# The low half of every fourth weight chunk: a ScalarE copy and an accumulating DMA in place of a VectorE subtraction

## The chip, the cores and the metric

The kernel runs on one core of a Trainium2 chip. A core has a matrix engine (TensorE; PE in the profile, its weight loads PEld), a vector engine (VectorE, DVE), a scalar engine (ScalarE, ACT), a general engine (GpSimd, POOL) and a queue engine (SyncE, SP). Each works through its own instructions in order; between engines only semaphores order the work. Sixteen DMA engines move data between the chip's main memory and the on-chip memory; SP, ACT and POOL can each hand transfers to them. The metric is device time in microseconds (us), the median of the runs, lower is better.

## The reference, cut to what matters

The reference is a two-layer decoder trunk on 256 tokens of width 2048, all in float32: layer 0 mixes retention heads with a short convolution, layer 1 is differential attention with two softmax maps per head, and each layer ends in a SwiGLU block of hidden width 5632.

```python
def swiglu(h, w_gate, w_up, w_down):
    return (jax.nn.silu(h @ w_gate) * (h @ w_up)) @ w_down
...
for layer in range(DEPTH):
    h = rms_norm(x, norm_mix[layer])
    x = x + (hybrid_retention_conv if layer % 2 == 0 else diff_attention)(h, ...)
    x = x + swiglu(rms_norm(x, norm_ffn[layer]), w_gate, w_up, w_down)
```

Nearly all arithmetic is in the products with weights: the input projection (2048 x 6144), the query-key-value projection (2048 x 6144), two output projections (2048 x 2048), and per layer gate, up (2048 x 5632 each) and down (5632 x 2048). Every weight is read once.

## The kernel before, in words

A product is cut into blocks of 512 output columns (`col_block`, L126). A block has two accumulators, one for each half of the 256 tokens, and walks along the contraction in **chunks** of 256 weight rows (two k-tiles of 128), so a block with 16 k-tiles has eight chunks (c0 = 0, 2, ... 14) and a chunk of weights is 128 partitions x 1024 numbers, 512 KB. The whole kernel has 784 chunks.

To keep float32 accuracy on a matrix engine that takes a shortened type (fp32r), activations and weights are split into a high part and a low part, and each product is made of three: high x high (L146), low activation x high weight (L147), high activation x low weight (L148). With two k-tiles and two token halves a chunk is 12 matmuls of 512 columns. The way of a chunk's weights is:

- SP issues a 1 MB load for two chunks into a `raw` buffer (L135). There are four such buffers, so a load waits until the chunks of the load four before it have been split.
- ACT writes the high part, `whi = cast(raw)` (L138). There are four `whi` buffers; the cast waits until PE has done the last matmul with the chunk four before.
- DVE writes the low part, `wlo = raw - whi` (L140), into one of four `wlo` buffers.
- PE runs the 12 matmuls (L146 to L148).

`wpool` hands its buffers out in turn, so chunks c0 = 2, 10 of a 16-tile block (every fourth chunk) always meet the same `whi` and the same `wlo` buffer. Small transposes and attention products run on PE between chunks; they come from a queue of jobs (`step`, L115). The names in the profile are block letters with `_raw`, `_hi`, `_lo`, `_a` (accumulator): `g` gate, `u` up, `d...` down, `n1o`, `n3o` output projections, `aq`, `ak`, `av` attention, `rq` to `cb` layer 0. `n_hi`, `n_lo`, `d0b_hi` are activations.

The instructions of each engine stand in the order that the program's scheduler gave them when the kernel was built; it may move an instruction ahead of another on its engine where data allow.

In attention POOL does a part of the rotary embedding: squares (L480), a power for the norm (L108) and four multiplications of 128x256 for each q or k (L491). Otherwise POOL is nearly empty.

Of the kernel before, what the change touches and what calls it, by code (L numbers as in the profile page):

```python
# [9 lines left out]
F32 = mybir.dt.float32  # L10
F32R = mybir.dt.float32r
AF = mybir.ActivationFunctionType
ALU = mybir.AluOpType
# [3 lines left out]
P = 128  # L17
# [4 lines left out]
NB = 512  # L22
KC = 2
KD = 4
# [11 lines left out]
def decoder_trunk(ctx: ExitStack, tc: tile.TileContext, a: dict):  # L36
    nc = tc.nc
# [5 lines left out]
    small = ctx.enter_context(tc.tile_pool(name="small", bufs=3))  # L43
# [5 lines left out]
    def tp_tile(name):  # L49
        return psum.tile([P, NB], F32, tag="tp", name=name, bufs=2)  # L50

# [1 line left out]
    ident = cpool.tile([P, P], F32, name="ident")  # L53
    x_sb = cpool.tile([P, NT, D], F32, name="x_sb")
    gcol = cpool.tile([P, 88], F32, name="gcol")
# [21 lines left out]
    def turn_gains(i, n):  # L77
# [8 lines left out]
        out=ident, in_=ident, compare_op=ALU.not_equal, fill=1.0, base=0,  # L86
# [13 lines left out]
            pattern=[[-1, P]], channel_multiplier=1,  # L100
        )

# [1 line left out]
    def rsqrt_mean(out, ss, n):  # L104
        """out = (ss / n + eps) ** -0.5 on small [P, w] tiles."""
        w = ss.shape[1]
        nc.vector.tensor_scalar(out, ss, 1.0 / n, EPS, ALU.mult, ALU.add)
        nc.gpsimd.tensor_tensor(out, out, mhalf[:, :w], ALU.pow)  # L108

    # Work that follows a product but holds the tensor engine runs between the chunks of the next  # L110
    # product: each job is a generator that yields where the tensor engine should go on meanwhile.
    jobs = deque()

    def step():
# [9 lines left out]
            step()  # L124

    def col_block(name, w, row0, n0, nk, hi, lo, kd=KD):  # L126
        """acc[t] = act[t] @ w[row0 : row0 + nk * P, n0 : n0 + NB], act split in hi + lo."""
        acc = [acc_tile(f"{name}_a{t}") for t in range(NT)]
        for c0 in range(0, nk, KC):
            if c0 % KD == 0:  # L130
                raw = wpool.tile([P, KD, NB], F32, tag="raw", name=f"{name}_raw{c0}", bufs=4)
            if c0 % kd == 0:
                k0 = row0 + c0 * P
                rows = w[k0 : k0 + kd * P, n0 : n0 + NB].rearrange("(k p) n -> p k n", p=P)
                nc.sync.dma_start(raw[:, c0 % KD : c0 % KD + kd], rows)  # L135
            part = raw[:, c0 % KD : c0 % KD + KC]
            whi = wpool.tile([P, KC, NB], F32R, tag="whi", name=f"{name}_hi{c0}")
            nc.scalar.copy(whi, part)  # L138
            wlo = wpool.tile([P, KC, NB], F32R, tag="wlo", name=f"{name}_lo{c0}")
            nc.vector.tensor_tensor(wlo, part, whi.bitcast(F32), ALU.subtract)  # L140
            for t in range(NT):
                ts = slice(t * P, (t + 1) * P)
                for j in range(KC):
                    k = c0 + j
                    first, last = k == 0, k == nk - 1
                    nc.tensor.matmul(acc[t], lhsT=hi[:, k, ts], rhs=whi[:, j], start=first, stop=False)  # L146
                    nc.tensor.matmul(acc[t], lhsT=lo[:, k, ts], rhs=whi[:, j], start=False, stop=False)  # L147
                    nc.tensor.matmul(acc[t], lhsT=hi[:, k, ts], rhs=wlo[:, j], start=False, stop=last)  # L148
            step()
        flush()  # L150
        return acc
# [4 lines left out]
        return hi, lo  # L156

    def split4(src, hi, lo, k0, t, name):
        """Transpose src [P tokens, 512] of token tile t into k-tiles k0 .. k0+3 of hi and lo."""
        pt = tp_tile(f"{name}_tp")  # L160
        for j in range(4):
            nc.tensor.transpose(pt[:, j * P : (j + 1) * P], src[:, j * P : (j + 1) * P], ident)
        pv = pt.rearrange("p (j s) -> p j s", j=4)
        ts = slice(t * P, (t + 1) * P)
        nc.scalar.copy(hi[:, k0 : k0 + 4, ts], pv)
        nc.vector.tensor_tensor(lo[:, k0 : k0 + 4, ts], pv, hi.bitcast(F32)[:, k0 : k0 + 4, ts], ALU.subtract)

    class Stream:
        """The residual stream's next normed activation: x * gain, transposed and split, with
        the row scale kept apart for the products' results."""  # L170

        def __init__(self, name, g0):
            self.name, self.g0 = name, g0
# [8 lines left out]
                nc.scalar.activation(junk, x_sb[:, t, cs], AF.Square, accum_out=self.ss[:, t, c : c + 1])  # L182

        def pair(self, q):
            """k-tiles 2q and 2q + 1."""
            pt = tp_tile(f"{self.name}_tp{q}")
            for j in range(2):
                k = 2 * q + j
                for t in range(NT):
                    nc.tensor.transpose(  # L190
                        pt[:, j * S + t * P : j * S + (t + 1) * P], x_sb[:, t, k * P : (k + 1) * P], ident
                    )
            for j in range(2):
                k = 2 * q + j
                g = gcol[:, self.g0 + k : self.g0 + k + 1]
                pv = pt[:, j * S : (j + 1) * S]
                nc.scalar.activation(self.hi[:, k], pv, AF.Copy, scale=g)
                nc.vector.scalar_tensor_tensor(
                    self.lo[:, k], pv, g, self.hi.bitcast(F32)[:, k], op0=ALU.mult, op1=ALU.subtract
                )  # L200
# [27 lines left out]
            nc.vector.tensor_tensor(x_sb[:, t, cs], acc[t], x_sb[:, t, cs], ALU.add)  # L228

    def rope(psum_in, r, cos, sin, out, h, hd, name):  # L230
        """out = rope(r * in) for h heads of hd columns; sin's first half carries the minus."""
        half = hd // 2
        v = psum_in.rearrange("p (h d) -> p h d", d=hd)
        ca = work.tile([P, h, hd], F32, tag="ropeA", name=name + "_A")
        cb = work.tile([P, h, hd], F32, tag="ropeB", name=name + "_B")
        nc.vector.scalar_tensor_tensor(
            ca, v, r, cos.unsqueeze(1).to_broadcast([P, h, hd]), op0=ALU.mult, op1=ALU.mult
        )
        for i in range(2):
            o, s = slice(i * half, (i + 1) * half), slice((1 - i) * half, (2 - i) * half)  # L240
            nc.vector.scalar_tensor_tensor(
                cb[:, :, o], v[:, :, s], r, sin[:, o].unsqueeze(1).to_broadcast([P, h, half]),
                op0=ALU.mult, op1=ALU.mult,
            )
        nc.gpsimd.tensor_tensor(out.rearrange("p (h d) -> p h d", d=hd), ca, cb, ALU.add)

    def transpose4(src, dst, t, name):
        """src [P tokens, 512] -> dst[:, 0:4, tokens of t], float32."""
        pt = tp_tile(f"{name}_tp")
        for j in range(4):  # L250
            nc.tensor.transpose(pt[:, j * P : (j + 1) * P], src[:, j * P : (j + 1) * P], ident)
        nc.scalar.copy(dst[:, :, t * P : (t + 1) * P], pt.rearrange("p (j s) -> p j s", j=4))
# [10 lines left out]
            yield  # L263
            split4(srcs[t], hi, lo, k0, t, f"{name}{t}")

# [1 line left out]
    st = Stream("n0", 0)  # L267
    st.pair(0)
    jobs.append(st.whole())
# [16 lines left out]
    for nm, n0, dst in (("rq", 0, qT), ("rk", 512, kT)):  # L286
        acc = proj(nm, n0, KC if n0 == 0 else KD)
# [39 lines left out]
    for half in range(2):  # L327
        acc = proj(f"rv{half}", 1024 + half * NB)
# [5 lines left out]
        acc = proj(f"rg{half}", 2048 + half * NB)  # L334
# [39 lines left out]
    for half in range(2):  # L374
        acc = proj(f"cc{half}", 4096 + half * NB)
# [3 lines left out]
        acc = proj(f"cx{half}", 5120 + half * NB)  # L379
# [3 lines left out]
        acc = proj(f"cb{half}", 3072 + half * NB)  # L383
# [45 lines left out]
    st, r = out_proj("n1", a["hyb_w_out"][0], KT, ca_hi, ca_lo, 32)  # L429
    st, r = ffn(0, st, r, 16)  # L430

# [1 line left out]
    cosa = work.tile([P, NT, AD], F32, tag="ropeA", name="cosa")  # L433
    sina = work.tile([P, NT, AD], F32, tag="ropeB", name="sina")
    nc.scalar.dma_start(cosa, a["cosa"].rearrange("(t p) d -> p t d", p=P))
# [34 lines left out]
    scale = AD ** -0.5  # L470

    def rotary(i, nm, acc, grp):
        """Norm and rotary embedding of four heads' q or k; returns both token tiles."""
        ct, sn = tabs[i]
        rots = []
        for t in range(NT):
# [20 lines left out]
        return rots  # L497

    def softmax(grp, hh, aq, ak):
        """The weights p0 / sum0 - lam * p1 / sum1 of one head: [queries, keys] of both query tiles."""  # L500
        nm = f"{grp}{hh}"
        sc = psum.tile([P, 2, NB], F32, tag="sc", name=f"asc{nm}")
        for m in range(2):
# [103 lines left out]


def _tables():
    """Rotary tables and decays: they depend on the shapes alone."""  # L610
    import numpy as np

    f32 = np.float32
    out = {}
    for nm, dim in (("r", RDK), ("a", AD)):
        inv = (f32(10000.0) ** (-np.arange(0, dim, 2, dtype=f32) / f32(dim))).astype(f32)
        ang = (np.arange(S, dtype=f32)[:, None] * inv[None, :]).astype(f32).astype(np.float64)
        c, s = np.cos(ang), np.sin(ang)
        out["cos" + nm] = np.concatenate([c, c], 1).astype(f32)
        out["sin" + nm] = np.concatenate([-s, s], 1).astype(f32)  # L620
    gamma = f32(1.0) - np.exp2(f32(-5.0) - np.arange(RH, dtype=f32)).astype(f32)
    log_g = np.log(gamma.astype(np.float64)).astype(f32).astype(np.float64)
    dist = np.arange(S)[None, :] - np.arange(P)[:, None]
    dec = np.where(dist >= 0, np.exp(log_g[:, None, None] * np.maximum(dist, 0)), 0.0) * RDK ** -0.5
    dec = dec.transpose(1, 0, 2)
    out["decay"] = np.ascontiguousarray(dec.reshape(P, RH * S)).astype(f32)
    return out
# [23 lines left out]
```

## Time and profile before

| | |
|---|---|
| median of 2 runs | 2235.55 us (2235.45 to 2235.66) |
| span of the profiled execution, first to last instruction | 2233.8 us |
| PE busy | 2224.0 us (100%) |
| DVE, ACT, POOL busy | 1235.7 (55%), 996.0 (45%), 115.8 us (5%) |
| DMA | 418.90 MB, mean 188 GB/s |
| granted TensorE clock | 1.000 |

The span is of one profiled execution, on its own clock from the first to the last instruction; the profile gives no other time for that execution. It is 1.75 us under the median. Matmuls overlap in the records (one lasts 390 ns, but the next starts after 227 ns), so PE's pace is read from starts.

### The profile page before, as it was taken

What the parts mean: (1) busy time and instruction counts of PE and PEld (TensorE: products, weight loads), DVE (VectorE), ACT (ScalarE), POOL (GpSimd) and SP (SyncE); (2) the same over time, 40 slices, a digit from 0 to 9 for tenths busy, and PEclk for the clock granted to TensorE, in tenths of its full rate; (3) what the DMA queues carried; (4) which work ended last, traced back from release to release, by engine and by line L of the source; (5) the groups of instructions that cost most, each with busy time, mean ns of one, the idle gap of its engine ahead of it and who ended that gap; (6) DMA issues with size and microseconds to landing.
All of it is one profiled execution on the core that took longest, in us unless ns stands there. A gap on an engine that the chain in (4) does not pass through costs nothing.

```text
span 2233.8 us, 25353 instructions
## 1 busy us (share of the span) xinstructions
PE 2224.0 (100%) x10115; PEld 1842.8 (82%) x10115; DVE 1235.7 (55%) x1320; ACT 996.0 (45%) x1172; POOL 115.8 (5%) x104
## 2 busy tenths in 40 slices
PE   8999999999999999999999999999999999999999
PEld 7888888888888888888888888888888888888887
DVE  5555565544554555455677778665445544554554
ACT  5444445444334443444545545554444344434443
POOL 1110000000000000000031233000000000000000
PEclk9999999999999999999999999999999999999999
DMA  8555555555565655555555555555555656555553
GB/s 286 174 180 188 191 186 188 189 189 189 189 197 192 193 190 188 189 189 188 188 177 164 188 170 170 170 188 189 189 189 189 194 190 193 191 192 189 188 188 132
DMA packets 212860, 418.90 MB, mean 188 GB/s; under 512 B 7341, under 2 KB 10885, under 8 KB 212613
## 3 DMA queue, kind: packets, MB, share of 16 engines
q1 hardware_dynamic: 209904, 414.34, 56.7%
q10 hardware_dynamic: 2836, 2.93, 0.4%
q8 instruction: 79, 1.29, 0.2%
q14 instruction: 41, 0.33, 0.0%
HBM read 415.15 MB, written 2.10 MB: 187 GB/s over the span
## 4 chain that ended last, share of the span: by engine, by line
PE 99%; DMA 1%; ACT 0%; DVE 0%; SPq 0%; issue 0%
PE g_a L146 7%; PE g_a L148 7%; PE g_a L147 7%; PE u_a L146 7%; PE u_a L147 7%; PE u_a L148 7%; PE av_a L148 1%; PE av_a L146 1%; PE ak_a L148 1%; PE n3o_a L147 1%; PE ak_a L147 1%; PE n3o_a L146 1%; PE aq_a L147 1%; PE aq_a L148 1%; PE n3o_a L148 1%; PE n1o_a L148 1%
## 5 line engine op out<-in xcount | busy, mean ns | idle before, releaser
L140 DVE TENSOR_TENSOR u_lo<-u_raw,u_hi 128x1024 fp32r<-128x1024 f32 x176 | 215.6, 1225 | 263.0 <-ACT u_hi L138 263.0
L140 DVE TENSOR_TENSOR g_lo<-g_raw,g_hi 128x1024 fp32r<-128x1024 f32 x176 | 215.6, 1225 | 226.5 <-ACT g_hi L138 224.8
L138 ACT CAST g_hi<-g_raw 128x1024 fp32r<-128x1024 f32 x176 | 185.5, 1054 | 287.3 <-PE g_a L147 139.9
L138 ACT CAST u_hi<-u_raw 128x1024 fp32r<-128x1024 f32 x176 | 185.6, 1055 | 252.0 <-PE u_a L147 132.9
L146 PE MATMUL g_a<-g_hi,n_hi 128*128 128x512 f32 x704 | 277.3, 394 | 0.0
L148 PE MATMUL g_a<-g_lo,n_hi 128*128 128x512 f32 x704 | 274.4, 390 | 0.0
L147 PE MATMUL g_a<-g_hi,n_lo 128*128 128x512 f32 x704 | 273.9, 389 | 0.0
L146 PE MATMUL u_a<-u_hi,n_hi 128*128 128x512 f32 x704 | 273.9, 389 | 0.0
L147 PE MATMUL u_a<-u_hi,n_lo 128*128 128x512 f32 x704 | 273.9, 389 | 0.0
L148 PE MATMUL u_a<-u_lo,n_hi 128*128 128x512 f32 x704 | 273.9, 389 | 0.0
L148 PEld LDWEIGHTS g_a<-g_lo,n_hi 128*128 128x128 f32 x704 | 132.1, 188 | 28.1
L148 PEld LDWEIGHTS u_a<-u_lo,n_hi 128*128 128x128 f32 x704 | 132.2, 188 | 27.5
L146 PEld LDWEIGHTS u_a<-u_hi,n_hi 128*128 128x128 f32 x704 | 132.2, 188 | 27.4
L147 PEld LDWEIGHTS u_a<-u_hi,n_lo 128*128 128x128 f32 x704 | 132.2, 188 | 27.4
L147 PEld LDWEIGHTS g_a<-g_hi,n_lo 128*128 128x128 f32 x704 | 132.3, 188 | 26.5
L146 PEld LDWEIGHTS g_a<-g_hi,n_hi 128*128 128x128 f32 x704 | 132.2, 188 | 26.2
L140 DVE TENSOR_TENSOR d11o_lo<-d11o_raw,d11o_hi 128x1024 fp32r<-128x1024 f32 x32 | 39.2, 1225 | 42.2 <-ACT d11o_hi L138 42.1
L140 DVE TENSOR_TENSOR d00o_lo<-d00o_raw,d00o_hi 128x1024 fp32r<-128x1024 f32 x32 | 39.2, 1225 | 42.2 <-ACT d00o_hi L138 42.1
L140 DVE TENSOR_TENSOR d01o_lo<-d01o_raw,d01o_hi 128x1024 fp32r<-128x1024 f32 x32 | 39.2, 1225 | 42.2 <-ACT d01o_hi L138 42.1
L140 DVE TENSOR_TENSOR d10o_lo<-d10o_raw,d10o_hi 128x1024 fp32r<-128x1024 f32 x32 | 39.2, 1225 | 42.2 <-ACT d10o_hi L138 42.1
L140 DVE TENSOR_TENSOR n1o_lo<-n1o_raw,n1o_hi 128x1024 fp32r<-128x1024 f32 x32 | 39.4, 1232 | 35.6 <-ACT n1o_hi L138 35.6
L138 ACT CAST d10o_hi<-d10o_raw 128x1024 fp32r<-128x1024 f32 x32 | 33.8, 1055 | 53.3 <-PE d10o_a L147 46.6
(305 smaller groups left out, 4594.1 us busy)
## 6 DMA issues: line engine op xcount, KB each, us to landing
g_raw<-in_ffn_w_gate_dram SPq DMA_DIRECT2D x88, 1024.0 KB, 5.2
u_raw<-in_ffn_w_up_dram SPq DMA_DIRECT2D x88, 1024.0 KB, 5.2
n1o_raw<-in_hyb_w_out_dram SPq DMA_DIRECT2D x16, 1024.0 KB, 5.1
d00o_raw<-in_ffn_w_down_dram SPq DMA_DIRECT2D x16, 1024.0 KB, 5.1
d01o_raw<-in_ffn_w_down_dram SPq DMA_DIRECT2D x16, 1024.0 KB, 5.1
aq_raw<-in_diff_w_qkv_dram SPq DMA_DIRECT2D x16, 1024.0 KB, 5.1
ak_raw<-in_diff_w_qkv_dram SPq DMA_DIRECT2D x16, 1024.0 KB, 5.1
av_raw<-in_diff_w_qkv_dram SPq DMA_DIRECT2D x16, 1024.0 KB, 5.1
```

The lines of the kernel that those rows point to most:

```text
L138: nc.scalar.copy(whi, part)
L140: nc.vector.tensor_tensor(wlo, part, whi.bitcast(F32), ALU.subtract)
L146: nc.tensor.matmul(acc[t], lhsT=hi[:, k, ts], rhs=whi[:, j], start=first, stop=False)
L147: nc.tensor.matmul(acc[t], lhsT=lo[:, k, ts], rhs=whi[:, j], start=False, stop=False)
L148: nc.tensor.matmul(acc[t], lhsT=hi[:, k, ts], rhs=wlo[:, j], start=False, stop=last)
```

## The change

For every chunk with c0 % 8 == 2 (c0 = 2 and 10 of a block with 16 k-tiles, and of a block with 12), the subtraction on DVE is left out. ACT writes `wlo = -whi` after its cast, and POOL issues a DMA that reads the same 512 KB of weights from main memory a second time and adds them to what stands in `wlo`. These are 200 of the 784 chunks. The other 584 are as before. Comments and docstrings were deleted as well, which moves later lines: the subtraction is now L145, the matmuls L151 to L153, the new copy L142 and the new DMA L143; the load (L135) and the cast (L138) keep theirs.

```diff
@@ col_block
             whi = wpool.tile([P, KC, NB], F32R, tag="whi", name=f"{name}_hi{c0}")
             nc.scalar.copy(whi, part)
             wlo = wpool.tile([P, KC, NB], F32R, tag="wlo", name=f"{name}_lo{c0}")
-            nc.vector.tensor_tensor(wlo, part, whi.bitcast(F32), ALU.subtract)
+            if c0 % (2 * KD) == KC:
+                rows = w[row0 + c0 * P : row0 + (c0 + KC) * P, n0 : n0 + NB]
+                nc.scalar.mul(wlo, whi.bitcast(F32), -1.0)
+                nc.gpsimd.dma_start(wlo, rows.rearrange("(k p) n -> p k n", p=P), accum_op=ALU.add)
+            else:
+                nc.vector.tensor_tensor(wlo, part, whi.bitcast(F32), ALU.subtract)
```

The scheduler orders the instructions anew. On PE, chunk c0 = 10 of an up block (`u05`; the first number in a name is the layer and block, the second the chunk) began before with

```order
L146 MATMUL u05_a0_5006<-u05_hi10_5094,n1_hi_2154 128x512 [waits Activation_49]
L147 MATMUL u05_a0_5006<-u05_hi10_5094,n1_lo_2155 128x512
L148 MATMUL u05_a0_5006<-u05_lo10_5096,n1_hi_2154 128x512 [waits DVE_49]
L146 MATMUL u05_a0_5006<-u05_hi10_5094,n1_hi_2154 128x512
L147 MATMUL u05_a0_5006<-u05_hi10_5094,n1_lo_2155 128x512
```

and now begins with

```order
L151 MATMUL u05_a0_5068<-u05_hi10_5157,n1_hi_2178 128x512 [waits Activation_49]
L152 MATMUL u05_a0_5068<-u05_hi10_5157,n1_lo_2179 128x512
L151 MATMUL u05_a1_5069<-u05_hi10_5157,n1_hi_2178 128x512
L152 MATMUL u05_a1_5069<-u05_hi10_5157,n1_lo_2179 128x512
L153 MATMUL u05_a0_5068<-u05_lo10_5159,n1_hi_2178 128x512 [waits DMASW7_49]
L151 MATMUL u05_a0_5068<-u05_hi10_5157,n1_hi_2178 128x512
```

The first matmul that needs the low part stands fifth instead of third, and waits for the new DMA (DMASW) instead of DVE. On ACT the same chunk now reads

```order
L138 CAST u05_hi10_5157<-u05_raw8_5139 128x1024 [waits PE_49,Activation_49]
L142 ACTIVATE u05_lo10_5159<-u05_hi10_5157 128x1024 [waits DMASW6_49,PE_49,Activation_49]
L138 CAST u05_hi12_5176<-u05_raw12_5174 128x1024 [waits DMAHW2_49,DVE_49,PE_49]
```

where before the two casts followed each other. On POOL in attention, around group 0's query multiplications, the order now is

```order
L496 TENSOR_TENSOR aqB00_7999<-aqsb00_7988,rtab_7802 128x4x64 [waits DVE_49]
L496 TENSOR_TENSOR aqB00_7999<-aqsb00_7988,rtab_7802 128x4x64 [waits Pool_49]
L496 TENSOR_TENSOR aqB01_8016<-aqsb01_8005,rtab_7802 128x4x64 [waits DVE_49]
L496 TENSOR_TENSOR aqB01_8016<-aqsb01_8005,rtab_7802 128x4x64
L143 DMA ak0_lo10_8125<-in_diff_w_qkv_dram 128x2x512 [waits DMASW6_49,Activation_49]
```

where the four multiplications had nothing behind them but the next squares. Five DMAs stand behind four such multiplications (`ak0_lo10` and the `lo10` of `av0` to `av3`); elsewhere POOL's order is DMA after DMA.

## Rows read from the trace of the kernel before

**Rows 1.** Page, busy time by engine, and what PE waited for (total, times, longest).

```profile
PE 2224.0 (100%) x10115; PEld 1842.8 (82%) x10115; DVE 1235.7 (55%) x1320; ACT 996.0 (45%) x1172; POOL 115.8 (5%) x104
...
PE ptg L79 <- DMA grow<-in_norm_mix_dram: 4.1, 1, 4.1
PE n_tp L190 <- DVE n_lo L198: 1.1, 1, 1.1
PE rq_a L147 <- DVE n_lo L198: 0.5, 2, 0.3
```

**Rows 2.** Page, the chain that ended last, by engine.

```profile
PE 99%; DMA 1%; ACT 0%; DVE 0%; SPq 0%; issue 0%
```

**Rows 3.** Timeline of ACT, 705 to 716 us: start, length, instruction, [idle before, releaser].

```profile
706.36 1.05 ACT L138 CAST u_hi<-u_raw 128x1024 fp32r<-128x1024 f32 x1 [1.67 <-PE g_a L147]
709.08 1.05 ACT L138 CAST u_hi<-u_raw 128x1024 fp32r<-128x1024 f32 x1 [1.67 <-PE g_a L147]
711.79 1.05 ACT L138 CAST u_hi<-u_raw 128x1024 fp32r<-128x1024 f32 x1 [1.67 <-PE g_a L147]
713.38 0.69 ACT L408 ACTIVATE gs<-g_a,n_r 128x512 f32<-128x512 f32 x1 [0.53 <-PE g_a L148]
```

**Rows 4.** Timelines of PE, DVE and SP in the same stretch.

```profile
706.15 0.39 PE L148 MATMUL g_a<-g_lo,n_hi 128*128 128x512 f32 x1
706.38 0.39 PE L146 MATMUL g_a<-g_hi,n_hi 128*128 128x512 f32 x1
...
707.44 1.22 DVE L140 TENSOR_TENSOR u_lo<-u_raw,u_hi 128x1024 fp32r<-128x1024 f32 x1 [1.49 <-ACT u_hi L138]
...
705.98 0.37 SPq L135 DMA_DIRECT2D u_raw<-in_ffn_w_up_dram  x1
711.41 0.37 SPq L135 DMA_DIRECT2D g_raw<-in_ffn_w_gate_dram  x1
```

**Rows 5.** Chain in order of time, transposes between chunks: start, length.

```profile
1085.90 0.87 PE d0b_tp L190 x8
```

**Rows 6.** DMA issues: count, KB each, median us from issue to landing.

```profile
u_raw<-in_ffn_w_up_dram SPq DMA_DIRECT2D x88, 1024.0 KB, 5.2
out_dram<-x_sb ACTq DMA_DIRECT2D x8, 256.0 KB, 2.2
cosa<-in_cosa_dram ACTq DMA_DIRECT2D x1, 128.0 KB, 2.1
sina<-in_sina_dram ACTq DMA_DIRECT2D x1, 128.0 KB, 2.7
rtab<-in_diff_subln_dram ACTq DMA_DIRECT2D x1, 128.0 KB, 2.9
rk_raw<-in_hyb_w_in_dram SPq DMA_DIRECT2D x4, 1024.0 KB, 11.7
```

**Rows 7.** Page, DMA queue of SP: packets, MB, share of 16 engines' span.

```profile
q1 hardware_dynamic: 209904, 414.34, 56.7%
```

**Rows 8.** Busy by stretch: PE, PEld, DVE, ACT, POOL, granted clock, DMA share, GB/s.

```profile
0.00:60.00 60.00, 54.22 (x242) 43.45 (x243) 35.57 (x50) 34.12 (x56) 7.88 (x13) 1.00 0.82 283
60.00:200.00 140.00, 140.00 (x668) 115.96 (x667) 73.03 (x79) 64.42 (x71) 14.81 (x11) 1.00 0.56 178
```

**Rows 9.** Timeline of POOL in attention.

```profile
1142.97 1.31 POOL L108 TENSOR_TENSOR aqrr<-aqrr,mhalf 128x4 f32<-128x4 f32 x1 [0.97 <-DVE aqrr L107]
1144.26 4.71 POOL L491 TENSOR_TENSOR aqB<-aqsb,rtab 128x256 f32<-128x256 f32 x4
...
1163.66 1.01 POOL L108 TENSOR_TENSOR akrr<-akrr,mhalf 128x4 f32<-128x4 f32 x1
1208.54 0.70 POOL L108 TENSOR_TENSOR ro<-ro,mhalf 128x2 f32<-128x2 f32 x1 [36.91 <-DVE ro L107]
```

**Rows 10.** Timeline of ACT in attention, the cast of `ak` chunk 10 in group 0.

```profile
1142.85 1.05 ACT L138 CAST ak_hi<-ak_raw 128x1024 fp32r<-128x1024 f32 x1 [1.66 <-DVE aqrr L107]
```

## The prediction, made before the changed kernel was run

> **What bounds the kernel now.** I read the busy shares first. PE is busy for 2224.0 of 2233.8 us, and all its waits together come to 4.1 + 1.1 + 0.5 = 5.7 us [rows 1]; the chain that ended last is 99% PE [rows 2]. So nothing that shortens DVE's, ACT's or the DMA's work can give back more than about 6 us (0.3%), and the DVE work that the change takes away lies wholly beside PE. The question is only whether the new way of a low part is late.
>
> For that I read one steady stretch. ACT's casts follow each other every 2.72 us, each released by PE's last use of the buffer four chunks before [rows 3]; 2.72 us is 12 matmuls, 0.227 us each, which is also the distance of two starts on PE [rows 4]. I take the start of a cast as zero of a clock for its chunk. At 706.36 the cast starts and at 706.38 PE starts the next chunk [rows 3, 4]: so from zero PE has three other chunks to do, 36 matmuls, before this one. Before the change the low part was needed after two more, at 38 x 0.227 = 8.6 us, and was ready at 707.44 + 1.22 - 706.36 = 2.3 us [rows 4]: 6.3 us of slack.
>
> **The change, part by part.**
>
> *The subtraction.* 200 DVE instructions of 1.22 us [rows 4], 244 us, go. DVE had slack; gain on the path: nothing, at most the 1.6 us for which PE ever waited for DVE [rows 1].
>
> *The deadline.* In the new order the first matmul with the low part is the fifth of its chunk, so the deadline is 40 x 0.227 = 9.07 us. Counting matmuls in the order of the changed program from one use of the same buffer to the next, 120 of the 200 chunks have this deadline and 2 have about 8; for 65 small PE work stands in between, mostly eight transposes, 0.87 us [rows 5], so they have 9.3 to 10.2, taken as 9.9; some 12 have more than 11.
>
> *ACT.* Cast 1.05 us, then the new copy. An ACTIVATE of half the size takes 0.69 [rows 3]; between the cast's 1.05 and twice 0.69 I take 1.1, since the cast has the new copy's shape. 200 x 1.1 = 220 us more on ACT, which is 45% busy: hidden, except that ACT finishes at 2.15 instead of 1.05.
>
> *The issue on POOL.* No row shows POOL issuing a DMA. Low end: SP's issue, 0.37 [rows 4]; high end: POOL's slowest small operation, 1.31, with 0.70 and 1.01 beside it [rows 9]. POOL's own short operations are nearest; I take 1.0.
>
> *The transfer, without its data.* 128 KB on a second queue beside the weight loads took 2.1, 2.7 and 2.9 us [rows 6]. The middle one, less 0.37 for the issue and about 0.4 for the data, is 1.9. Low end: the line through 256 KB in 2.2 and 1024 KB in 5.2 [rows 6] starts at 1.2, which is 0.8 without the issue; high end: 2.9 - 0.8 = 2.1.
>
> *The data.* SP's queue took 56.7% of 16 engines' span for 209904 packets [rows 7]: 0.567 x 2233.8 x 16 / 209904 = 0.0965 us a packet of 2 KB. A transfer of 512 KB is 16 packets per DMA engine, 1.54 us. This DMA must read its destination as well as its source. If a packet costs what it did, 1.54; if the second read is paid in full, 3.1. I take 3.1, because each byte written now has two bytes read through the same engine. At a copy's price the sum below would be 1.6 us less, 7.9, and the wait would be gone. The Trainium skill (Collectives: The Full Stack, "Why ReduceScatter is half of AllGather") lets an adding transfer run at half the rate of a copy, for its two reads; no run here shows it yet.
>
> *The collision.* The 1 MB load that reuses the same `raw` buffer no longer waits for DVE but for this very cast: SP issues it at 1.05, and it lands 5.2 later [rows 6], at 6.2. The new DMA has its data on the move from about 2.15 + 1.0 + 1.2 = 4.35. About 1.8 us of the load are left then, of which some 0.5 are its ending; the 16 engines serve both queues, so I add 1.3. Low end nothing, high end 1.8. Where queues are full, a 1 MB load took 11.7 us [rows 6]; that is the far end for the whole transfer.
>
> *Sum for one chunk:* 2.15 + 1.0 + 1.9 + 3.1 + 1.3 = 9.45 us, against 9.07. PE then waits 0.38 us in 122 chunks, and not at all in those with 9.9: 46 us. The wait repeats, because PE's last use of a `wlo` buffer releases the next chunk of the same kind, so it is not absorbed.
>
> *POOL in attention.* Five of the DMAs stand behind four multiplications. The cast of `ak` chunk 10 starts at 1142.85 [rows 10], so its DMA could start at 1145.0; the multiplications end at 1144.26 + 4.71 = 1148.97 [rows 9], 4.0 us later. 9.45 + 4.0 - 9.9 = 3.5 us of waiting, five times: 18 us.
>
> *The start.* In the first 60 us the DMA engines are 82% busy [rows 8]. Five new transfers of 3.1 us are 15.5 us of engine time; 10.8 are free: 5 us.
>
> *What is queued behind the new waits.* ACT's copy waits for PE's release of `wlo`, one matmul after that of `whi`, while the cast still runs: nothing. POOL's DMA waits for ACT; behind it stand other DMAs, and in attention the rotary work, which a job two chunks later uses: hidden. SP's loads start 1.2 us earlier and have the cover of about six chunks. DMA in all: 56.7% plus 200 x 3.1 / 2233.8 = 28% is 85%: below full.
>
> Together 46 + 18 + 5 = 69 us on the profiled 2233.8 gives 2303; the median of the runs stands 1.75 above the span: **2305 us**, 3% slower.
>
> **The rivals.** The sum lies close to its deadline, so the cases are told by when the low part is ready. Two per cent, about what a measurement of this kernel can tell from no change, is 45 us; it is reached at 9.25 us (122 x 0.18 + 23).
>
> *Not slower: the transfer is hidden.* All low ends, 2.1 + 0.37 + 0.8 + 1.54, give 4.8 us; the late DMAs in attention then reach 8.8 and are hidden too, and only the start costs up to 5 us: about 2238. Up to 9.25 us the time stays under 2280. For it: every term has a low end that suffices, and one or two of them are enough. Against it: POOL's small operations are all slow. The Trainium skill (DMA: Bandwidth & Descriptors, "Anatomy of one DMA") gives for a transfer issued from POOL an estimate of 2.0 us plus bytes at 436 GB/s, 3.2 us for these 512 KB; by that rule the low part is ready at 5.4 us and this rival is right. No row has such a transfer, and the page's fit is for plain copies. Chance 0.38.
>
> *Much slower: the addition sets the rate.* If an adding packet takes four packet times instead of two, the data take 6.2 us and the low part is ready at 12.55: 122 x 3.5 + 65 x 2.65 + 20 in attention and 11 elsewhere are about 630 us, 2865 us. It decides from about 11 us on (2560 us); by engine time alone DMA would then be 57% + 55%, over full. Nothing in the trace speaks for or against, as no DMA here adds. Chance 0.17.
>
> *Faster.* It would have to come out of the 5.7 us of waits; under 2% in any case. A chance of 0.01 for what I do not see.
>
> **How the numbers follow.** The forecast, 9.25 to 11 us or 2280 to 2560 us, has 0.44. Slower by over 2%: 0.44 + 0.17 = 0.61; within: 0.38; faster: 0.01. The range runs from the hidden case, 2234 (its few us of cost left out), to 2560, and leaves out the upper rival. The forecast's own range is 2280 to 2560.
>
> **What would show it.** In the profile after: ACTIVATE at L142 near 1.1 us, 200 times; the time to landing of the `_lo` DMAs, 7.3 us by my terms counted from the issue; PE waiting for those DMAs at L153, about 0.4 us each in the blocks without transposes before the chunk, and several us at `ak0` and `av`; DVE near 990 us busy; the DMA share near 85%. If PE shows no such waits and the DMAs land within 6 us, the hidden case was right; if they land after 9 us, the addition is slow. I would be wrong altogether if matmuls themselves ran at another pace.

## The result and the profile after

The changed kernel takes **2314.85 us** (median of 2 runs, 2313.79 to 2315.91) where the kernel before takes 2235.55: a ratio of **1.0355, 95% interval 1.0325 to 1.0385**, 79 us slower. The forecast was 2305. Its profiled execution has a span of 2312.0 us, 78.2 more than before.

The page of the changed kernel, busy time by engine, queues, and the chain that ended last; these lines answer to [rows 1], [rows 7] and [rows 2]:

```profile
PE 2256.1 (98%) x10115; PEld 1838.5 (80%) x10115; DVE 1000.2 (43%) x1120; ACT 1209.4 (52%) x1372; POOL 344.2 (15%) x304
...
q1 hardware_dynamic: 209904, 414.34, 55.2%
q0 software_dynamic: 54400, 104.87, 26.2%
...
PE 71%; DMA 19%; ACT 6%; issue 2%; POOL 1%; DVE 1%; ACTq 0%; POOLq 0%
```

DVE has lost its 236 us and ACT has gained 213: both lay beside PE and moved nothing. What counts is the chain: it was 99% PE, and now 19% of it runs through DMAs and 6% through ACT. That is the new path of a low part, cast, copy, adding DMA, which PE waits for. What PE waited for, by the longest totals (engine, line, releaser: total us, times, longest):

```profile
PE n_tp L195 <- issue: 8.3, 2, 4.6
PE av_a L153 <- DMA av_lo<-in_diff_w_qkv_dram: 5.6, 8, 1.6
PE u_a L153 <- DMA u_lo<-in_ffn_w_up_dram: 5.2, 10, 0.9
PE ptg L79 <- DMA grow<-in_norm_mix_dram: 4.3, 1, 4.3
PE n3o_a L153 <- DMA n3o_lo<-in_diff_w_out_dram: 3.4, 3, 2.5
PE g_a L153 <- DMA g_lo<-in_ffn_w_gate_dram: 2.8, 5, 0.7
PE d0bo_a L153 <- DMA d0bo_lo<-in_ffn_w_down_dram: 2.6, 2, 1.4
```

Before, the list held 5.7 us in all [rows 1]. Now nearly every block has a line at L153, the matmuls with the low weights (L148 before), each a few us in waits of some tenths. The first line is another matter: it is the start, below.

One wait, followed link by link, in timelines of ACT, POOL and PE and in the chain (start, length, what):

```profile
752.87 1.05 ACT L138 CAST u_hi<-u_raw 128x1024 fp32r<-128x1024 f32 x1 [1.72 <-PE u_a L152]
753.95 1.06 ACT L142 ACTIVATE u_lo<-u_hi 128x1024 fp32r<-128x1024 f32 x1
```

```profile
755.31 1.21 POOL L143 DMA_DIRECT2D u_lo<-in_ffn_w_up_dram  x1 [9.66 <-ACT u_lo L142]
```

```profile
755.31 7.39 DMA u_lo<-in_ffn_w_up_dram
```

```profile
761.45 0.39 PE L151 MATMUL u_a<-u_hi,n_hi 128*128 128x512 f32 x1
761.68 0.39 PE L152 MATMUL u_a<-u_hi,n_lo 128*128 128x512 f32 x1
762.74 0.50 PE L153 MATMUL u_a<-u_lo,n_hi 128*128 128x512 f32 x1 [0.67 <-DMA u_lo<-in_ffn_w_up_dram]
763.07 0.40 PE L151 MATMUL u_a<-u_hi,n_hi 128*128 128x512 f32 x1
```

With the cast at 752.87 as zero: the copy ends at 2.14, POOL's instruction starts at 2.44, the DMA has landed at 9.83. PE would have started the L153 matmul at 761.68 + 0.227 = 761.91, which is 9.04 on that clock (9.07 forecast); it starts at 762.74, 0.83 us late. The matmul behind it comes another 0.10 late (0.33 after its neighbour instead of 0.227).

Over all 200 low parts, counted from the trace (median, with the 10th and 90th percentile): ready 9.23 us after the start of the cast (8.81, 10.13), mean 9.38; issue to landing 6.77 us (6.27, 7.55), of which the first packet 2.86 after the issue, the data 3.66, the ending 0.32. Landing times by issue, medians in the last column, answer to [rows 6]:

```profile
u_raw<-in_ffn_w_up_dram SPq DMA_DIRECT2D x88, 1024.0 KB, 5.2
u_lo<-in_ffn_w_up_dram POOLq DMA_DIRECT2D x44, 512.0 KB, 6.5
av_lo<-in_diff_w_qkv_dram POOLq DMA_DIRECT2D x8, 512.0 KB, 6.9
rq_lo<-in_hyb_w_in_dram POOLq DMA_DIRECT2D x2, 512.0 KB, 8.4
```

Where the lateness gathers is told by how much later the same cast starts than before, counted from the two traces: 9.3 us at the first cast of `rk`, 11.7 at that of `rv` (50 us into the kernel before, 62 into the changed one), 24.0 at the first of `g` (374 and 398 us), 45.0 at `ak`, 54.4 at `n3o`, 77.9 at the end. So 11.7 us are lost in the first 60, 9.4 in attention from `ak` on (11.1 if it is counted at the first matmuls of the same blocks), and the other 57 come bit by bit. The waits at L153 add up to about 49 us over some 100 events, with a median of 0.3.

**The start.** Stretches of the changed kernel, and under them the same of before (PE, PEld, DVE, ACT, POOL busy, granted clock, DMA share, GB/s):

```profile
0.00:60.00 60.00, 45.33 (x191) 36.50 (x192) 24.05 (x39) 33.96 (x56) 11.42 (x16) 0.91 0.90 279
...
14.50:24.00 9.50, 1.30 (x11) 0.85 (x8) 5.72 (x12) 6.64 (x18) 0.35 (x1) 0.76 1.10 335
24.00:30.00 6.00, 5.87 (x19) 4.98 (x20) 2.27 (x6) 2.69 (x5) 0.37 (x1) 0.52 1.02 386
```

```profile
14.50:24.00 9.50, 9.34 (x48) 7.42 (x47) 7.62 (x12) 8.71 (x18) 0.71 (x1) 1.00 1.06 378
24.00:30.00 6.00, 5.71 (x30) 4.40 (x29) 3.19 (x7) 2.96 (x5) 0.00 (x0) 1.00 1.05 387
```

From 14.5 to 24 us PE now does 1.30 us of work instead of 9.34, and after that its granted clock is 0.52, the lower of its two levels (1.2 of 2.4 GHz). What PE waits for there, from its timeline and ACT's:

```profile
14.14 0.60 PE L195 MATMUL n_tp<-ident,x_sb 128*128 128x128 f32 x4
18.43 1.06 PE L195 MATMUL n_tp<-ident,x_sb 128*128 128x128 f32 x8 [3.69 <-issue]
24.14 1.94 PE L195 MATMUL n_tp<-ident,x_sb 128*128 128x128 f32 x8 [4.64 <-issue]
25.73 0.78 PE L153 MATMUL rq_a<-rq_lo,n_hi 128*128 128x512 f32 x1
26.30 0.63 PE L151 MATMUL rq_a<-rq_hi,n_hi 128*128 128x512 f32 x1
26.73 0.63 PE L152 MATMUL rq_a<-rq_hi,n_lo 128*128 128x512 f32 x1
```

```profile
21.82 0.63 ACT L187 ACTIVATE n_j<-x_sb 128x512 f32<-128x512 f32 x1 [1.82 <-DMA x_sb<-in_x_dram]
```

In the scheduler's new order the transposes of all remaining pieces of the input (`n_tp`) stand ahead of the matmuls that need the first low part (`rq_lo`, chunk 2); before, those transposes stood between the matmuls of later chunks. Why it chose this order is not shown. So PE has nothing in its order but transposes, these wait for their buffers and so for ACT, and ACT for the last load of x. `rq_lo` itself, issued at 11.76 and landed at 21.2, would have held PE up too: the first matmul with it stood at 13.44 before. How much of the loss is the order and how much the late low part, no run separates. Two waits of 3.7 and 4.6 us and some ten matmuls at 0.427 instead of 0.227 us make the start.

### The profile page after: what moved, and what is told of

Read it like the earlier page. It is cut to its first block, busy times and chain, and to the rows that moved or that the text cites. A ratio compares the mean times of both kernels' runs of the same rounds, so it can differ in the third digit from the quotient of the medians.

```text
span 2312.0 us, 25745 instructions
## 1 busy us (share of the span) xinstructions
PE 2256.1 (98%) x10115; PEld 1838.5 (80%) x10115; DVE 1000.2 (43%) x1120; ACT 1209.4 (52%) x1372; POOL 344.2 (15%) x304
## 3 DMA queue, kind: packets, MB, share of 16 engines
q0 software_dynamic: 54400, 104.87, 26.2%
## 4 chain that ended last, share of the span: by engine, by line
PE 71%; DMA 19%; ACT 6%; issue 2%; POOL 1%; DVE 1%; ACTq 0%; POOLq 0%
PE u_a L153 6%; PE g_a L153 6%; PE g_a L152 6%; PE g_a L151 6%; PE u_a L152 5%; PE u_a L151 5%; DMA u_lo<-in_ffn_w_up_dram 4%; DMA g_lo<-in_ffn_w_gate_dram 2%; DMA d01o_lo<-in_ffn_w_down_dram 2%; DMA d10o_lo<-in_ffn_w_down_dram 1%; DMA d00o_lo<-in_ffn_w_down_dram 1%; PE aq_a L153 1%; PE aq_a L152 1%; PE aq_a L151 1%; DMA av_lo<-in_diff_w_qkv_dram 1%
## 5 line engine op out<-in xcount | busy, mean ns | idle before, releaser
L138 ACT CAST g_hi<-g_raw 128x1024 fp32r<-128x1024 f32 x176 | 185.3, 1053 | 236.5 <-PE g_a L152 106.3
L145 DVE TENSOR_TENSOR u_lo<-u_raw,u_hi 128x1024 fp32r<-128x1024 f32 x132 | 161.8, 1225 | 328.6 <-ACT u_hi L138 328.6
L138 ACT CAST u_hi<-u_raw 128x1024 fp32r<-128x1024 f32 x176 | 185.3, 1053 | 215.9 <-PE u_a L152 114.8
L145 DVE TENSOR_TENSOR g_lo<-g_raw,g_hi 128x1024 fp32r<-128x1024 f32 x132 | 161.7, 1225 | 287.6 <-ACT g_hi L138 285.9
L153 PE MATMUL u_a<-u_lo,n_hi 128*128 128x512 f32 x704 | 269.8, 393 | 5.6 <-DMA u_lo<-in_ffn_w_up_dram 5.2
L151 PE MATMUL g_a<-g_hi,n_hi 128*128 128x512 f32 x704 | 274.2, 389 | 0.0
L151 PE MATMUL u_a<-u_hi,n_hi 128*128 128x512 f32 x704 | 274.2, 389 | 0.0
L153 PE MATMUL g_a<-g_lo,n_hi 128*128 128x512 f32 x704 | 270.1, 394 | 2.9 <-DMA g_lo<-in_ffn_w_gate_dram 2.8
L153 PEld LDWEIGHTS u_a<-u_lo,n_hi 128*128 128x128 f32 x704 | 132.1, 188 | 42.9 <-DMA u_lo<-in_ffn_w_up_dram 15.3
L153 PEld LDWEIGHTS g_a<-g_lo,n_hi 128*128 128x128 f32 x704 | 132.1, 188 | 35.3 <-DMA g_lo<-in_ffn_w_gate_dram 8.4
L151 PEld LDWEIGHTS u_a<-u_hi,n_hi 128*128 128x128 f32 x704 | 132.2, 188 | 26.4
L151 PEld LDWEIGHTS g_a<-g_hi,n_hi 128*128 128x128 f32 x704 | 132.2, 188 | 26.2
L143 POOL DMA_DIRECT2D g_lo<-in_ffn_w_gate_dram x44 | 53.0, 1204 | 438.6 <-ACT g_lo L142 438.6
L143 POOL DMA_DIRECT2D u_lo<-in_ffn_w_up_dram x44 | 53.0, 1204 | 437.3 <-ACT u_lo L142 437.3
L138 ACT CAST d01o_hi<-d01o_raw 128x1024 fp32r<-128x1024 f32 x32 | 33.7, 1053 | 47.3 <-PE d01o_a L152 41.7
L138 ACT CAST d10o_hi<-d10o_raw 128x1024 fp32r<-128x1024 f32 x32 | 33.7, 1053 | 46.9 <-PE d10o_a L152 41.3
L138 ACT CAST d11o_hi<-d11o_raw 128x1024 fp32r<-128x1024 f32 x32 | 33.7, 1053 | 46.8 <-PE d11o_a L152 41.3
L138 ACT CAST d00o_hi<-d00o_raw 128x1024 fp32r<-128x1024 f32 x32 | 33.7, 1053 | 46.4 <-PE d00o_a L152 40.8
```

The lines of the kernel that those rows point to most:

```text
L143: nc.gpsimd.dma_start(wlo, rows.rearrange("(k p) n -> p k n", p=P), accum_op=ALU.add)
```

## The experiments

Lateness is counted as above, against the kernel before; "ready" is the time from a cast's start to the landing of its low part.

**Five buffers** for each half instead of four, with three for the raw weights to make room:

```diff
-  raw = wpool.tile([P, KD, NB], F32, tag="raw", ..., bufs=4)
+  raw = wpool.tile([P, KD, NB], F32, tag="raw", ..., bufs=3)
-  whi = wpool.tile([P, KC, NB], F32R, tag="whi", ...)
+  whi = wpool.tile([P, KC, NB], F32R, tag="whi", ..., bufs=5)
-  wlo = wpool.tile([P, KC, NB], F32R, tag="wlo", ...)
+  wlo = wpool.tile([P, KC, NB], F32R, tag="wlo", ..., bufs=5)
```

> The changed kernel with five whi and five wlo buffers instead of four, and three raw buffers instead of four to make room. Theory (the low part lands after its deadline): the deadline moves from 9.07 to 11.3 us (50 matmuls: the low part is third of its chunk again), while the low part is ready at 9.2 in the median and 10.1 at the ninetieth percentile; PE's waits at L153, 49 us in all, fall under 10, and 2245 to 2262 us remain (the start and attention). Rival (DMA load): the transfers slow the kernel through the DMA engines, 82% busy; then the time stays within 10 us of 2315. Rival (ACT): the extra 1.06 us copy delays the casts; also stays near 2315.

Measured: 2249.2 us (2249.1 to 2252.0), ratio to before 1.0065 (1.005 to 1.008). The low parts are as late as in the change (ready 9.29, DMA engines as busy), but the deadline is a chunk further off, and the waits at L153 fall from about 49 to 5 us. What PE still waited for:

```profile
PE n_tp L195 <- issue: 8.8, 2, 5.1
PE ptg L79 <- DMA grow<-in_norm_mix_dram: 4.3, 1, 4.3
PE n3o_a L153 <- DMA n3o_lo<-in_diff_w_out_dram: 1.5, 2, 1.2
```

Of some 14 us left, 8.0 are the start by the casts. But with five buffers a cast is released one chunk (2.72 us) earlier, which makes it look less late than PE is. Counted at the first matmuls of the blocks, PE is 11.2 us late at `rv`, stays at 11.2 to 11.3 until `n3o`, and loses 2 more there: nearly all that is left is the start. So the loss is one of lateness against a deadline: the extra work on ACT, POOL and the DMA engines is all still there and costs little.

**The DMA without its addition** (it overwrites the negated copy, so the low half is not computed):

```diff
-  nc.gpsimd.dma_start(wlo, rows.rearrange(...), accum_op=ALU.add)
+  nc.gpsimd.dma_start(wlo, rows.rearrange(...))
```

> The DMA from POOL overwrites the low part with the weights instead of adding to it (what is computed is not the product any more); all else is as in the change, the same 512 KB, queue and waits. Theory (the second read is the term that passes the deadline): a packet falls from 188 ns to near the 100 ns of the raw loads, the data from 3.7 to about 2.2 us, the low part is ready at 7.8 instead of 9.3 us, the waits at L153 fall from 49 to under 8 us and the time to 2245 to 2262. Rival (the queue from POOL is what is slow, whatever it carries): packets stay at 170 ns or more and the time stays within 10 us of 2315.

Measured: 2252.86 us (2251.0 to 2253.5), 1.0077 (1.0062 to 1.0092). Ready is 7.77 us, the data take 2.26 instead of 3.66, a 2 KB packet 107 ns instead of 188. The queue's line on the page, beside the 26.2% of the change for the same packets:

```profile
q0 software_dynamic: 54400, 104.87, 15.5%
```

The addition makes a packet 81 ns longer, three quarters of a plain one. POOL's own instruction is also shorter here (0.71 us instead of 1.20), which makes little difference to the first packet (2.68 us after its start instead of 2.86). The waits at L153 are 5.2 us, the start still costs 9.5. The 1.5 us that the addition costs are what lies between hidden and not.

**The same DMAs beside the old way**: copy and adding DMA go to a spare buffer that nothing reads, and DVE subtracts in every chunk as before.

```diff
-  nc.scalar.mul(wlo, whi.bitcast(F32), -1.0)
-  nc.gpsimd.dma_start(wlo, rows.rearrange(...), accum_op=ALU.add)
- else:
-  nc.vector.tensor_tensor(wlo, part, whi.bitcast(F32), ALU.subtract)
+  spare = wpool.tile([P, KC, NB], F32R, tag="spare", ..., bufs=1)
+  nc.scalar.mul(spare, whi.bitcast(F32), -1.0)
+  nc.gpsimd.dma_start(spare, rows.rearrange(...), accum_op=ALU.add)
+nc.vector.tensor_tensor(wlo, part, whi.bitcast(F32), ALU.subtract)
```

(with three raw buffers, as above)

> The negated copy and the adding DMA go to a spare buffer that nobody reads, and VectorE does the subtraction for every chunk as before; raw has three buffers to make room. Same load on ACT, POOL and the DMA engines as in the change, but PE waits for none of it. Theory: PE is not held up, 2236 to 2246 us (some of the start). Rival (DMA load or ACT load as such): 2290 or more. It also shows what three raw buffers cost in e1_bufs5: by the theory nothing.

Measured: 2237.09 us (2236.7 to 2237.6), 1.0008 (0.9998 to 1.0017). Busy time and queues on its page, and its first 60 us:

```profile
PE 2224.8 (100%) x10115; PEld 1842.8 (82%) x10115; DVE 1238.0 (55%) x1320; ACT 1200.4 (54%) x1372; POOL 356.4 (16%) x304
...
q1 hardware_dynamic: 209904, 414.34, 56.8%
q0 software_dynamic: 54400, 104.87, 26.8%
```

```profile
0.00:60.00 60.00, 53.66 (x236) 42.63 (x237) 35.15 (x47) 37.54 (x61) 12.62 (x17) 1.00 0.94 292
```

All the added work is done and costs next to nothing (1.7 us); PE doesn't wait for it. In the first 60 us the DMA engines are even busier (0.94) than in the change (0.90), and PE is not held up: DMA time is not what the start costs. This run also shows something about queues. Its raw load is issued about 2.3 us after the cast (behind DVE), together with the adding DMA, and the first adding packet comes 4.59 us after POOL's issue instead of 2.86. Counted from the traces, medians in us after POOL's issue of the DMA:

| kernel | eight tenths of the load's packets ended | first packet of POOL's DMA |
|---|---|---|
| the change | 2.62 | 2.86 |
| without the addition | 2.49 | 2.68 |
| beside the old way | 4.27 | 4.59 |
| adding from SBUF (below) | 0.46 | 1.44 |
| other chunks (below) | 1.14 | 1.92 |

Where a load is ahead, POOL's DMA starts when it is nearly through; where it is through early, after 1.4 to 1.9 us. POOL's instruction itself takes 0.71 us without the addition, 0.86 from SBUF and 1.20 in the others; counted from its end, the first packet comes after 1.66, 1.98, 3.39, 0.57 and 0.72 us, so the picture stays.

**Adding from SBUF**: the DMA reads the `raw` buffer instead of main memory, so the buffer's next load waits until it has landed.

```diff
-  nc.gpsimd.dma_start(wlo, rows.rearrange(...), accum_op=ALU.add)
+  nc.gpsimd.dma_start(wlo, part, accum_op=ALU.add)
```

> The adding DMA takes the weights from the raw buffer on the chip instead of reading them from main memory again. So the next load into that raw buffer can only be issued after the DMA has landed. Theory (in the change the first packet starts 2.9 us after the issue because it stands behind the 1 MB load that the same cast released): that load is gone from before it, the first packet comes about 1.6 us after the issue, the data take 2.9 us without company, the low part is ready near 7.6 us; PE's waits at L153 fall from 49 us to under 10 and the time to 2243 to 2260. Rival (2.9 us are what POOL's queue needs to start): the first packet stays at 2.6 us or more after the issue, the low part at 8.5 or later, and the time above 2275.

Measured: 2262.13 us (2258.1 to 2263.6), 1.0117 (1.0102 to 1.0132), 2 us over the range expected. First packet 1.44 us after the issue, data 2.88, ready 7.35 us: the deadline is met in the steady stretch. What is left:

```profile
PE n_tp L195 <- DVE n_lo L203: 4.1, 1, 4.1
PE n_tp L195 <- issue: 4.0, 1, 4.0
PE ptg L79 <- DMA grow<-in_norm_mix_dram: 4.0, 1, 4.0
PE d0bo_a L153 <- DMA d0bo_lo<-d0bo_raw: 3.8, 2, 2.4
```

The start is again 10.4 us late, and another 10.4 are lost from `aq` to `n3o` (counted at the first matmuls). Three things differ here, the source, its packets (4 KB instead of 2) and the load that is out of the way, and this run alone doesn't separate them.

**No adding DMA in the first two blocks:**

```diff
-  if c0 % (2 * KD) == KC:
+  if c0 % (2 * KD) == KC and name not in ("rq", "rk"):
```

> The change without its DMA in the first two blocks (q and k of layer 0): four chunks are split on VectorE as before. Theory (11.7 of the 79 us are lost in the first 60 us, where PE starves behind the first low part and its clock falls to half): 11 to 13 us less than the change, 2302 to 2305. Rival (the start is late because the DMA engines are full, with whatever transfers): at most 4 us less.

Measured: 2307.54 us (2303.8 to 2308.8), 1.032 (1.0305 to 1.0336), 2.5 us over the range expected. The start is whole: lateness at `rv` is -0.4 us, the clock 1.00 in the first 60 us. But only 7.3 us of the 11.7 arrive at the end; the other blocks lost 4 to 5 us more than in the change. About 3 us of that are the clock: in this trace it falls to its lower level twice more, for 3.4 us each, from 1477.6 us (in `n3o`) and from 2272.9, which it doesn't do there in the change. For the rest, that a kernel less late by one wait comes upon other alignments of loads and casts would explain it, but isn't shown. So the start's share, as a part of the sum, holds to within those 5 us.

**Both cures**, five buffers and no adding DMA in `rq` and `rk`:

> The new low parts of the change, with five buffers for each half (three for the raw weights) and none in the blocks rq and rk: both cures together. Theory: the 79 us are short buffers (a low part ready 9.2 us after its cast, needed at 9.07) plus a start in which PE's order puts the transposes of the input ahead of matmuls that wait for the first low part. Five buffers alone left 13.7 us, of which 8.0 stood in the first 60 us; without the DMAs in rq and rk that start was gone. So 2249.2 - 8 = 2241 us, 2237 to 2246, with granted clock 1.00 in the first 60 us and about 5 us of PE waits in all. Rival, the start is only put off (leaving rq and rk out alone gave back 7.3 of 11.7 us, the rest was lost later): 2245 to 2250, with the lateness growing after rv. Rival, the added ACT, POOL and DMA work itself costs PE a few us: 2249 again, spread over the whole run.

Measured: 2239.03 us (2237.4 to 2240.7), 1.0016 (1.0006 to 1.0026). The clock is 1.00 throughout, and the list of PE's waits has come down to these lines, the first of which is there before as well [rows 1]:

```profile
PE ptg L79 <- DMA grow<-in_norm_mix_dram: 4.2, 1, 4.2
PE n3o_a L153 <- DMA n3o_lo<-in_diff_w_out_dram: 2.3, 2, 1.5
PE n_tp L195 <- DMA x_sb<-in_x_dram: 1.0, 1, 1.0
```

That is 10.2 us under five buffers alone, which fits the 11.2 that the start costs there at PE's matmuls and not the 8 read from the casts. Of 79 us, 3.4 are left, with 196 of the 200 low parts still made by the DMA, and still ready at 9.25. The two causes together account for the loss. The rival that the start is only put off, which the run before it suggested, falls where the deadline is kept.

**Other chunks**, c0 = 0 and 8, the first of the two that share a raw buffer, so that the cast releases no load:

```diff
-  if c0 % (2 * KD) == KC:
+  if c0 % (2 * KD) == 0:
```

> The adding DMA serves chunks c0 = 0 and 8 instead of 2 and 10, the first of a raw buffer's two instead of the second; as many chunks, nothing else changed. The weights still come from main memory. By the theory of the collision the load of 1 MB is now issued 0.4 us before the cast instead of 1.05 after it, its packets are through at about 4.1 instead of 5.6 us, the low part is ready near 8.0 instead of 9.2 us, and the waits at L153 fall under 20 us; the start may cost as much as before: 2248 to 2280. Rival (no collision; the transfer is as long wherever it stands): within 10 us of 2315.

Measured: 2288.67 us (2286.4 to 2289.6), 1.0237 (1.0222 to 1.0252), above the range expected. In the steady part the mechanism is as expected: the first packet comes 1.92 us after the issue instead of 2.86, with main memory as the source; ready is 8.60, and the feed-forward blocks wait hardly at all (0.3 and 0.8 us for all `g` and `u`). The loss moved, most of it to `n3o`:

```profile
PE n3o_a L153 <- DMA n3o_lo<-in_diff_w_out_dram: 9.4, 3, 3.7
PE n_tp L195 <- DVE n_lo L203: 6.0, 3, 4.3
PE ptg L79 <- DMA grow<-in_norm_mix_dram: 4.3, 1, 4.3
PE cc_a L153 <- DMA cc_lo<-in_hyb_w_in_dram: 4.0, 1, 4.0
```

With these waits the granted clock falls: it is at its lower level for 37 us in six stretches, 10 of them at the start and 17 in `n3o` (0.50 there from 1460.3, 1477.3 and 1501.2 us). From starts every 0.427 instead of 0.227 us that costs, as an estimate, up to 18 us of the 53.

The same without `rq` and `rk`:

> As the run on chunks c0 = 0 and 8, but without the DMA in the first two blocks. By the theory of the start (PE starves behind the first low parts) this takes away the 8 to 12 us of the start and leaves 2238 to 2262 us; if the start is not the first low parts, it is as the run on c0 = 0 and 8. It should not beat the kernel before, whose PE waits for 6 us in all.

Measured: 2273.32 us (2271.6 to 2280.2), 1.0179 (1.0161 to 1.0196), again above the range. It is 15.4 us under the run before it, and its lateness at `rv` is 0.1: the start again. Of the rest, 13.6 us are lost in `n3o` alone, counted at the first matmuls of the blocks. The trace puts three waits on `n3o_lo` there, 9.5 us beyond PE's pace (8.8 by its list). With the end of the two longest, of 3.4 and 2.8 us, the granted clock is 0.51 and 0.50 for 3.4 us each, and the slower matmuls cost another 2.9 us, so 12.4 of the 13.6 have their place. Why the low part is late just there (a change of blocks lies near) is not shown.

**Twice as many**, every second chunk:

```diff
-  if c0 % (2 * KD) == KC:
+  if c0 % KD == KC:
```

> Twice as many chunks (c0 % 4 == 2, 392 of 784) go by the adding DMA. By engine time: 209904 packets of 100 ns and 100352 of 188 ns on 16 DMA engines are 1312 + 1179 = 2491 us, so the DMA engines become the bound: 2500 to 2650 us, with a DMA share above 0.95. Rival (only the deadline counts, engine time does not): the loss doubles, 2380 to 2410 us, with a share near 1.05 x 0.82.

Measured: 2675.15 us (2668.5 to 2681.8), 1.1967 (1.1933 to 1.2002), above both ranges. The page:

```profile
PE 2372.0 (89%) x10115; PEld 1887.3 (70%) x10115; DVE 771.5 (29%) x928; ACT 1388.6 (52%) x1564; POOL 564.8 (21%) x496
...
q1 hardware_dynamic: 209904, 414.34, 46.5%
q0 software_dynamic: 106624, 205.55, 45.5%
```

Here the DMA engines are 92% busy over the span: one adding packet still takes 193 ns, but the DMAs are behind each other and ready at 10.46 in the median. The clock falls too: it is at its lower level for some 213 us, in stretches of 3.4 to 10 us all over the run, which by starts every 0.427 instead of 0.227 us is, as an estimate, up to 100 of the 440 us lost. So with 392 low parts the DMA engines are nearly full, with 200 they are not the limit; what part of the loss here is engine time, what lateness and what clock, this run doesn't separate.

## Why the prediction was right, point by point

The time, 2314.85 for 2305, came out by the mechanism forecast for most of the loss: a low part ready a few tenths of a us after PE wants it. The terms are less even than their sum, and that it came within 10 us is in part luck: the start was 7 us too small and by another mechanism, attention 7 to 9 too large, and among the terms of the ready time the errors of the transfer, the hand-over and the data cancel as well. The ready time itself came out at 9.23 us, just under the 9.25 where the prediction lets the time reach 2280: by its own conversion that is 122 x 0.16 + 23 = 43 us, or 2278. The step from the median to the wait was too cheap, and the spread, the restarts and the larger start made up for it.

- **What bounds the kernel.** Right: the 236 us taken from DVE gave nothing back.
- **The deadline**, 9.07 us: held (9.04 in the piece shown); a fifth buffer took the waits away.
- **Copy and issue.** 1.06 for 1.1 us. POOL's issue takes 1.20 (1.0 forecast), and 0.30 pass between the copy's end and POOL's start, which the sum didn't have.
- **The transfer without its data**, 1.9 us: too large. In the run on other chunks, where no load is in the way, the first packet comes 0.72 us after the end of POOL's instruction, and the ending takes 0.33: about 1.05.
- **The data.** 3.66 us for 3.1. Near two packet times instead of one: 188 ns against 100.6 for the raw loads (counted from the trace, means), and 107 without the addition. By the Trainium skill (Collectives: The Full Stack, "Why ReduceScatter is half of AllGather") the adding step of a collective runs at half the rate of the copying one because it reads two sources; the trace agrees nearly, at 1.87 times the packet time of the loads and 1.76 times that of POOL's plain DMA. The remark that a copy's price would give 7.9 us and no wait was borne out by the run without addition: 7.77. The rival with four packet times is shown wrong.
- **The collision with the next load.** 1.3 us forecast as sharing. The trace shows a queue: the add's packets hardly start before the load's have ended. First packet after 2.86 us, and 1.92 where the load ahead is through in time, so some 0.9 us (the low part is ready 0.63 earlier there, as its data take 0.2 longer); in the kernel with the spare buffer, where the load is issued later, 4.59. The Trainium skill (DMA: Bandwidth & Descriptors, "Queues, rings and completion order") has each DMA engine take turns between queues, a packet at a time, typically of 9 to 17 descriptors. Whether the 2 KB packets of the profile are such packets or their parts, the traces don't tell, so they can't say whether that rule holds; that the two queues' packets hardly overlap here is measured.
- **Landing and ready**: 6.77 for 7.3, and 9.23 for 9.45. The Trainium skill's fit for a DMA from POOL (DMA: Bandwidth & Descriptors, "Anatomy of one DMA"), an estimate of 3.2 us that would have made the hidden case right, is far from both the adding DMA (6.77) and the plain one (5.30), each with a load ahead of it.
- **0.38 us in 122 chunks, 46 us.** Measured 57 outside the start and attention. 36.7 of that are waits at L153. The median is only 0.16 past the deadline; the waits come from the upper half of the spread (90th percentile 10.13), some 72 of them with a mean of 0.5 us, not 122 of 0.38. A further part is the matmul after a wait, about 0.1 us late each time, which the sum didn't have. Counted as delays of starts beyond PE's pace, these stretches lose 41.5 us at L153, 9.6 at the other two matmuls and 3.2 elsewhere, more than before. (Events at L151 alone add up to 16.1 us over the run, but the kernel before has 11 us at its two as well, against 21 now.)
- **Attention, 18 us: too large.** The five DMAs behind POOL's multiplications started 2.4 to 2.8 us after the copy instead of 0.3, not 4.0 late, and PE waited 6.6 us for them instead of 18; attention from `ak` on lost 9.4 in all (11.1 at the matmuls).
- **The start, 5 us: too small, and the wrong step.** It was reckoned as a lack of DMA time. The kernel with the spare buffer has the same transfers there and loses 1.3 us in all. What failed is the claim that only engine time counts there: the first low part came almost 8 us after it was due, the scheduler had put the transposes ahead of its users, and the clock fell behind the pause. Together that is 11.7 us; how they share it is not shown.

46 + 18 + 5 = 69 was forecast, 57 + 9 + 12 = 78 measured. The hidden case, at 0.38, lost by 1.5 us of data time; that it was near is shown by the plain DMA and by the fifth buffer.

## What to carry to other kernels

Where one engine is busy for the whole span, taking work from another gains nothing, and the only question is whether the new path is ready in time: write down the deadline (the time of a chunk, times the buffers less one, and the matmuls of the chunk itself that come first) and add up the path, hop by hop, with the queue that the transfer stands in. Copy and adding DMA took 8.2 us where the subtraction took 1.2; if such a path is wanted, give it one more buffer and keep it out of the first chunks, where nothing is in stock. When lateness is compared between kernels with different numbers of buffers, count it at the engine that is the limit, not at a step that a buffer releases. And look at the granted clock around waits of some us: where it falls, as in `n3o` above, the slower matmuls are paid on top of the pause.

## What the runs showed of the hardware

- An adding DMA of 512 KB takes 188 ns for a 2 KB packet, a plain one beside the same loads 107, the loads 100.6.
- An adding DMA behind a 1 MB load on another queue doesn't share the engines with it: first packet 2.86 us after POOL's issue with a load issued 1.4 us earlier, 4.59 with one issued at about the same time, and 1.44 to 1.92 where the load's packets were eight tenths through 1.1 us after the issue or sooner.
- After a pause in which PE did 1.30 us of work in 9.5, its granted clock was 0.52 for the next 6 us; a matmul started every 0.427 us instead of 0.227. In the run on other chunks without `rq` and `rk`, with the end of waits of 3.4 and 2.8 us it was 0.51 and 0.50 for 3.4 us each.
- POOL's instruction that issues a DMA of 512 KB took 1.20 us for an adding one from main memory, 0.86 for an adding one from SBUF and 0.71 for a plain one.
